# Matmul with layer norm: row tiles of A loaded as 64 KB pieces with rows 32 s + r on partition r, so that the block transposes write contiguously

## The chip, the core and the metric

The kernel runs on one core of one Trainium2 chip. The metric is the device time of one execution in microseconds (us), lower is better. The times shown are three runs of the kernel before, and one execution under the hardware profiler, from which all durations come.

## The reference

```python
m, k, n = 2048, 2048, 2048            # a, b, gamma, beta: float32
x = np.matmul(a, b)
mean = np.mean(x, axis=-1, keepdims=True)
var = np.var(x, axis=-1, keepdims=True)
normalized = (x - mean) / np.sqrt(var + eps)
return (gamma * normalized + beta).astype(np.float32)
```

Every row of the product is normalised over its 2048 columns.

## The kernel before

**Tiling.** A has 16 row tiles of 128 rows (i = 0 to 15), K has 16 tiles of 128 (kt), and the 2048 columns of the product are four blocks of 512 (q), each of them one PSUM bank. TensorE multiplies in fp16 (L132): the stationary operand is a 128x128 piece of A transposed, `at[i][:, kt, :]`, the moving one is `b16[:, kt, 512 columns]`. A tile of `at` has K on its partitions: partition p and index kt = 4c + t stand for k = 512 c + 4 p + t. B is loaded in the same order (`b_rows`, L65), so that a partition reads contiguous memory.

**The first four row tiles** (L257 to L363) are worked on while B arrives, K in two halves and the columns in two halves. Their A comes in 16 pieces of 256 KB (`load_first`, L88), is cast by VectorE (`cast_first`), turned by TensorE (`turn_first`) and copied out of PSUM by VectorE (`keep_first`). B comes in 32 pieces of 512 KB, cast half by VectorE and half by ScalarE. ScalarE puts the first half of a sum aside (`put_by`, L144), and VectorE adds the second half to it (`add_up`, L148).

**Row tiles 4 to 15** (L353 to L386) take another way for A, the one that is changed. `load_tile` (L108) loads half a row tile into a float32 buffer of [128, 8, 128] of the pool `firstp`, which has four buffers. One transfer goes to each of the four groups q of 32 partitions. In the view `a_pieces` (L66) the rows of a tile are split as 4 r + j with r on the partition; group q of 32 partitions holds columns 128 q to 128 q + 127 of each of the four stretches of 512 columns (c). Half h holds rows j = 2h and 2h + 1, all four c. ScalarE casts the half to fp16 (`cast_tile`, L116). VectorE's 32x32 block transposes (`transpose_part`, L123), four for each row tile, each with 512 elements on 128 partitions, turn it into `at[i]`: inside a group of 32 partitions a block of 32 rows by 32 columns is turned, the columns being every fourth one. Part j reads row j of every r and writes every fourth element of `at[i]`, over all 16 kt.

**Order of the work.** The order on every engine is the order of the program text (`manual_schedule`, L219): no planner changes it, and each engine works through its list in order. In the loop over row tiles (L370 to L385) VectorE does, for each tile i: the normalisation of tile i - 1 (`normalise`: `centre`, L165, reads the product in PSUM and frees the bank; `scale`, L171), then four times the statistics of a bank (`stats`, L140) followed by one transpose for tile i + 2, and up to i = 11 half of the normalisation of one of the first four tiles. PSUM has eight banks, so the banks of tile i are those of tile i - 2.

**Queues.** SP's queue carries first the pieces of A and B, then the halves of tiles 4 and 5 (L248 to L250), then gamma and beta (L251, L252), then the output (L192). The queue of GpSimd (POOL) carries the halves of tiles 6 to 15 (L253 to L255); each waits until the cast of an earlier tile has freed a buffer. In the compiled program the transfers of a queue go round over eight completion semaphores; a transfer waits for the one eight places before it to have landed.

Of the kernel before, what the change touches and what calls it, by code (L numbers as in the profile page):

```python
# [9 lines left out]
FP32 = mybir.dt.float32  # L10
# [5 lines left out]
def kernel(  # L16
# [18 lines left out]
    nc = tc.nc  # L35
    P = 128
    M, K = a.shape
    _, N = b.shape
# [10 lines left out]
    firstp = ctx.enter_context(tc.tile_pool(name="firstp", bufs=4))  # L49
# [13 lines left out]
    b16 = bpool.tile([P, n_kt, N], FP16)  # L63

    b_rows = b.rearrange("(c p t) n -> c t p n", p=P, t=4)  # L65
    a_pieces = a.rearrange("(i r j) (c q k) -> q i r (j c) k", r=32, j=4, c=4, q=4)  # L66

    bnst, x_of, mv_of, rs_of, at = {}, {}, {}, {}, {}
    a_in, b_in, t_of, tile_in, part = {}, {}, {}, {}, {}
# [36 lines left out]
        nc.vector.tensor_copy(at[g][:, ds(4 * c, 4), :], t_of[n])  # L106

    def load_tile(i, h, queue):  # L108
        f = firstp.tile([P, 8, P], FP32, tag="first", name=f"p{i}_{h}")
        for q in range(4):  # L110
            queue.dma_start(f[ds(32 * q, 32)], a_pieces[q, i][:, ds(8 * h, 8)])  # L111
        tile_in[i, h] = f

    def cast_tile(i, h):
        a16 = a16p.tile([P, 2, 4, P], FP16, tag="a16", name=f"a{i}_{h}")
        nc.scalar.copy(a16.rearrange("p j c k -> p (j c) k"), tile_in.pop((i, h)))  # L116
        tile_in[i, h] = a16

    def new_at(i):
        at[i] = atp.tile([P, n_kt, P], FP16, tag="at", name=f"at{i}")  # L120

    def transpose_part(i, j):
        nc.vector.transpose(  # L123
            at[i].rearrange("p ct (r j) -> p j ct r", j=4)[:, j],
            tile_in[i, j // 2][:, j % 2].rearrange("p c (k t) -> p c t k", t=4),
        )

    def bank(i, q):
# [90 lines left out]
    with tc.manual_schedule(engines=order):  # L219
# [28 lines left out]
        for i in (4, 5):  # L248
            for h in (0, 1):
                load_tile(i, h, nc.sync)  # L250
        nc.sync.dma_start(gamma_b, gamma.unsqueeze(0).to_broadcast([P, N]))  # L251
        nc.sync.dma_start(beta_b, beta.unsqueeze(0).to_broadcast([P, N]))  # L252
        for i in range(6, n_mt):  # L253
            for h in (0, 1):
                load_tile(i, h, nc.gpsimd)  # L255
# [13 lines left out]
        for n in range(KH):  # L269
            g, c = pieces[n]  # L270
# [83 lines left out]
        for h in (0, 1):  # L354
            cast_tile(4, h)
            transpose_part(4, 2 * h)
            transpose_part(4, 2 * h + 1)
# [7 lines left out]
        for c in range(4):  # L365
            if c % 2 == 0:
                cast_tile(5, c // 2)
            transpose_part(5, c)

        for i in range(G, n_mt):  # L370
            if i > G:
                normalise(i - 1)
            if i + 2 < n_mt:
                new_at(i + 2)
            for q in range(n_nb):
                bank(i, q)
                for t in range(n_kt):
                    mm(i, q, t)
                stats(i, q)
                if i + 2 < n_mt:  # L380
                    if q % 2 == 0:
                        cast_tile(i + 2, q // 2)
                    transpose_part(i + 2, q)
                if q == 3 and i < 3 * G:
                    normalise((i - G) // 2, (i - G) % 2)  # L385
# [32 lines left out]
```

## Time and profile before

| what | before |
|---|---|
| three runs | 252.91, 253.35, 253.96 us; median 253.35 us |
| profiled execution | 251.89 us, of which the span from the first to the last instruction is 250.1 us |
| TensorE (PE) busy | 233.6 us, 93% of the span, 1108 matmuls |
| VectorE (DVE) busy | 214.0 us, 86%, 354 instructions |
| ScalarE (ACT) busy | 58.4 us, 23% |
| GpSimd (POOL) busy | 49.2 us, 20% |
| transposes of L123 | 48, 1.28 to 1.35 us each |
| DMA | 52.6 MB, 210 GB/s over the span |

The page gives busy times of the engines, a picture of the span in 40 slices in which each digit is the busy share in tenths, and the chain of waits that ended last. The timeline of an engine has one line for an instruction or for some alike: start in us, length in us, engine, line of the code, operation, output <- inputs, shape, count, and in square brackets how long the engine had been idle and what ended that. An engine called SPq is SP's queue, and its lines are issues of transfers. Consecutive instructions of an engine overlap a little, so the distance between two starts is less than the length of one.

### The profile page before, as it was taken

The numbers are of one execution on the slowest core, as the hardware profiler recorded it, in microseconds if no ns is written. First come the engines' busy times: TensorE is split into PE (matmuls) and PEld (weight loads), VectorE is DVE, ScalarE is ACT, GpSimd is POOL, SyncE is SP. The second block draws the span as 40 slices with busy tenths as digits, with TensorE's granted clock in tenths as the row PEclk, the third lists the DMA queues.
The fourth block names the chain that finished last, engine by engine and source line by source line (L and its number), as shares of the span: only waits on it lengthen the run. The fifth ranks groups of instructions, "written<-read, shape, count | busy, mean of one in ns | idle before, by whom it ended". The sixth has DMA issues, their size and how long they took to land.

```text
span 250.1 us, 3093 instructions
## 1 busy us (share of the span) xinstructions
PE 233.6 (93%) x1108; PEld 106.4 (43%) x1108; DVE 214.0 (86%) x354; ACT 58.4 (23%) x91; POOL 49.2 (20%) x87
## 2 busy tenths in 40 slices
PE   7999999999999999999999999989979899999940
PEld 2444454444444444444444444434434344444410
DVE  1654454389999999999999999999999999999953
ACT  2225628542411321030300303011030303000010
POOL 0000000000722907051150703407042000000003
PEclk9999999999999999999999999999999999999996
DMA  6999999999999836458282852908448240404214
GB/s 196 393 390 401 402 404 408 409 368 172 226 281 235 211 95 226 145 201 221 86 235 101 241 178 109 308 33 238 154 161 259 88 168 3 168 0 168 120 48 168
DMA packets 20302, 52.62 MB, mean 210 GB/s; under 512 B 2880, under 2 KB 6976, under 8 KB 20032
## 3 DMA queue, kind: packets, MB, share of 16 engines
q1 hardware_dynamic: 16160, 41.16, 46.1%
q0 software_dynamic: 3840, 10.49, 16.7%
q10 hardware_dynamic: 288, 0.79, 0.9%
q8 instruction: 8, 0.13, 0.2%
q14 instruction: 6, 0.05, 0.1%
HBM read 35.65 MB, written 16.78 MB: 210 GB/s over the span
## 4 chain that ended last, share of the span: by engine, by line
DVE 56%; PE 28%; DMA 8%; issue 3%; ACT 2%; SPq 0%; DVEq 0%
DMA w_1_137<-in_b_dram 3%; DMA f_1_121<-in_a_dram 3%; DMA f_0_107<-in_a_dram 2%; DVE at_1489 L123 2%; DVE at_1259 L123 2%; DVE at_1719 L123 2%; DVE at_911 L123 2%; DVE at_1601 L123 2%; DVE at_1141 L123 2%; DVE at_1371 L123 2%; DVE at_1029 L123 2%; DVE at_861 L123 2%; DVE at_902 L123 2%; PE ps_0_1936 L132 1%; PE ps_3_2189 L132 1%
## 5 line engine op out<-in xcount | busy, mean ns | idle before, releaser
L111 POOL DMA_DIRECT2D p_0_221<-in_a_dram x4 | 2.5, 624 | 61.8 <-DMA p_0_209<-in_a_dram 61.8
L205 POOL TENSOR_TENSOR y_last<-y_last,gamma_b 128x512 f32<-128x512 f32 x1 | 1.3, 1266 | 54.2 <-ACT y_last L204 54.2
L132 PEld LDWEIGHTS <-at_1601 128*128 128x128 f16 x64 | 6.3, 98 | 9.1 <-issue 1.6
L132 PEld LDWEIGHTS <-at_1489 128*128 128x128 f16 x64 | 6.3, 98 | 8.7 <-issue 1.2
L132 PEld LDWEIGHTS <-at_1719 128*128 128x128 f16 x64 | 6.3, 98 | 8.7 <-issue 1.2
L132 PEld LDWEIGHTS <-at_1371 128*128 128x128 f16 x64 | 6.3, 98 | 8.0 <-issue 0.6
L132 PEld LDWEIGHTS <-at_911 128*128 128x128 f16 x64 | 6.3, 98 | 7.5
L132 PEld LDWEIGHTS <-at_1259 128*128 128x128 f16 x64 | 6.3, 98 | 7.5
L132 PEld LDWEIGHTS <-at_1935 128*128 128x128 f16 x64 | 6.3, 98 | 7.5
L132 PEld LDWEIGHTS <-at_902 128*128 128x128 f16 x64 | 6.3, 98 | 7.5
L132 PEld LDWEIGHTS <-at_1831 128*128 128x128 f16 x64 | 6.3, 98 | 7.5
L132 PEld LDWEIGHTS <-at_861 128*128 128x128 f16 x64 | 6.3, 98 | 7.5
L132 PEld LDWEIGHTS <-at_1141 128*128 128x128 f16 x64 | 6.3, 98 | 7.5
L132 PEld LDWEIGHTS <-at_1029 128*128 128x128 f16 x64 | 6.2, 98 | 7.6
L132 PEld LDWEIGHTS <-at_324 128*128 128x128 f16 x64 | 6.2, 98 | 7.5 <-issue 0.4
L132 PEld LDWEIGHTS <-at_323 128*128 128x128 f16 x64 | 6.2, 98 | 7.3
L132 PEld LDWEIGHTS <-at_322 128*128 128x128 f16 x64 | 6.2, 98 | 7.3
L227 PE MATMUL w_ps<-warm 128*128 128x512 f16 x20 | 7.4, 514 | 1.2 <-DVE warm L220 1.2
L132 PEld LDWEIGHTS <-at_321 128*128 128x128 f16 x64 | 5.9, 98 | 6.1 <-issue 0.7
L132 PE MATMUL ps_0_1832<-b_93,at_1601 128*128 128x512 f16 x16 | 3.6, 378 | 1.3 <-DVE u_0_1702 L165 1.3
L132 PE MATMUL ps_0_1720<-b_93,at_1489 128*128 128x512 f16 x16 | 3.6, 379 | 1.0 <-DVE u_0_1584 L165 1.0
L132 PE MATMUL ps_0_1936<-b_93,at_1719 128*128 128x512 f16 x16 | 3.6, 379 | 1.0 <-DVE u_0_1814 L165 1.0
(556 smaller groups left out, 613.5 us busy)
## 6 DMA issues: line engine op xcount, KB each, us to landing
gamma_b<-in_gamma_dram SPq DMA_DIRECT2D x1, 1024.0 KB, 10.5
beta_b<-in_beta_dram SPq DMA_DIRECT2D x1, 1024.0 KB, 15.6
w_0_105<-in_b_dram ACTq DMA_DIRECT2D x1, 512.0 KB, 5.1
w_0_111<-in_b_dram SPq DMA_DIRECT2D x1, 512.0 KB, 6.9
w_0_115<-in_b_dram SPq DMA_DIRECT2D x1, 512.0 KB, 7.8
w_0_119<-in_b_dram SPq DMA_DIRECT2D x1, 512.0 KB, 6.5
w_0_123<-in_b_dram SPq DMA_DIRECT2D x1, 512.0 KB, 7.5
w_0_127<-in_b_dram SPq DMA_DIRECT2D x1, 512.0 KB, 8.3
```

Source lines behind the costliest of these rows:

```text
L111: queue.dma_start(f[ds(32 * q, 32)], a_pieces[q, i][:, ds(8 * h, 8)])
L123: nc.vector.transpose(at[i].rearrange("p ct (r j) -> p j ct r", j=4)[:, j], tile_in[i, j // 2][:, j % 2].rearrange("p c (k t) -> p c t k", ...
L132: nc.tensor.matmul(x_of[i, q], at[i][:, kt, :], b16[:, kt, ds(q * NB, NB)], start=(kt == lo), stop=(kt == hi - 1),)
L205: nc.gpsimd.tensor_tensor(y, y, gamma_b[:, q3], AluOp.mult)
L227: nc.tensor.matmul(w_ps, warm[:, 0:P], warm, start=True, stop=True)
```

## The change

Rows of a tile are split as 32 s + r instead of 4 r + j, with r on the partition as before. Half h of a tile now holds stretches c = 2h and 2h + 1 of the columns, with all four s, instead of two values of j with all four c. The rows s and the stretches c don't merge into one dimension of the view, so each transfer brings one c: eight transfers of 64 KB for a half, instead of four of 128 KB; the contiguous piece in memory is 512 B in both. That makes 32 transfers instead of 16 on SP's queue and 160 instead of 80 on GpSimd's. A transpose now works on one c with all four s, reads with the same step of four elements as before, and writes runs of 32 adjacent elements; it fills four kt of `at[i]`, where a part before filled a quarter of every kt. The number of casts and transposes, their sizes and their places in the order stay.

```diff
-    a_pieces = a.rearrange("(i r j) (c q k) -> q i r (j c) k", r=32, j=4, c=4, q=4)
+    a_pieces = a.rearrange("(s r) (c q k) -> q c r s k", r=32, c=4, q=4)
...
     def load_tile(i, h, queue):
-        f = firstp.tile([P, 8, P], FP32, tag="first", name=f"p{i}_{h}")
-        for q in range(4):
-            queue.dma_start(f[ds(32 * q, 32)], a_pieces[q, i][:, ds(8 * h, 8)])
+        f = firstp.tile([P, 2, 4, P], FP32, tag="first", name=f"p{i}_{h}")
+        for c in (0, 1):
+            for q in range(4):
+                queue.dma_start(
+                    f[ds(32 * q, 32), c], a_pieces[q, 2 * h + c][:, ds(4 * i, 4)])
         tile_in[i, h] = f
 
     def cast_tile(i, h):
         a16 = a16p.tile([P, 2, 4, P], FP16, tag="a16", name=f"a{i}_{h}")
-        nc.scalar.copy(a16.rearrange("p j c k -> p (j c) k"), tile_in.pop((i, h)))
+        nc.scalar.copy(a16, tile_in.pop((i, h)))
         tile_in[i, h] = a16
...
-    def transpose_part(i, j):
+    def transpose_part(i, c):
         nc.vector.transpose(
-            at[i].rearrange("p ct (r j) -> p j ct r", j=4)[:, j],
-            tile_in[i, j // 2][:, j % 2].rearrange("p c (k t) -> p c t k", t=4),
+            at[i][:, ds(4 * c, 4), :].rearrange("p t (j r) -> p j t r", r=32),
+            tile_in[i, c // 2][:, c % 2].rearrange("p j (k t) -> p j t k", t=4),
         )
```

## The prediction

> **What bounds the kernel now.** I read first the busy rows of the page, then the timeline of TensorE (PE), then the chain of waits and the timeline of VectorE (DVE), last the queues that bring A. [...] The sum is made against the span and carried over to the median as a difference in us.
>
> ```profile
> PE   7999999999999999999999999989979899999940
> DVE  1654454389999999999999999999999999999953
> ```
>
> Both engines are full from slice 10 on (a slice is 6.25 us), so the busy rows don't say which one limits. TensorE's few 8s and the 7 after slice 10 lie between 150 and 200 us. The timeline of TensorE, one line per PSUM bank (start, length, engine, line, operation, idle time before it), shows what the dips are:
>
> ```profile
> 149.76 3.62 PE L132 MATMUL ps_3_1552<-b_93,at_1259 128*128 128x512 f16 x16
> 153.65 3.61 PE L132 MATMUL ps_0_1602<-b_93,at_1371 128*128 128x512 f16 x16 [0.27 <-DVE u_0_1472 L165]
> ...
> 164.00 3.62 PE L132 MATMUL ps_3_1664<-b_93,at_1371 128*128 128x512 f16 x16
> 168.58 3.61 PE L132 MATMUL ps_0_1720<-b_93,at_1489 128*128 128x512 f16 x16 [0.96 <-DVE u_0_1584 L165]
> ...
> 178.94 3.62 PE L132 MATMUL ps_3_1782<-b_93,at_1489 128*128 128x512 f16 x16
> 183.90 3.61 PE L132 MATMUL ps_0_1832<-b_93,at_1601 128*128 128x512 f16 x16 [1.34 <-DVE u_0_1702 L165]
> ...
> 194.25 3.62 PE L132 MATMUL ps_3_1894<-b_93,at_1601 128*128 128x512 f16 x16
> 198.83 3.40 PE L132 MATMUL ps_0_1936<-b_93,at_1719 128*128 128x512 f16 x15 [0.96 <-DVE u_0_1814 L165]
> ```
>
> Undisturbed banks start 3.453 us apart (13.81 us a row tile). The four starts shown are later than that by 0.44, 1.13, 1.51 and 1.13 us: **4.2 us in all**. Each time TensorE waits for VectorE's `centre` (L165) of the row tile two before, which frees the first of eight banks. The starts of that instruction lie at 92.37, 107.30, 122.60, 137.54, 152.84, 167.78, 183.09 and 198.03 us: 15.1 us a tile against TensorE's 13.8. So VectorE is the slower engine from about 90 to 198 us, uses up TensorE's lead of two tiles by 153 us, and from then on sets the pace. Before 153 and after 199 us TensorE runs on without a gap (3.45 us a bank up to 240.4). The whole that a faster VectorE can win is those 4.2 us.
>
> ```profile
> 158.19 0.69 DVE L140 BATCH_NORM_STATS2 bnst_1507<-ps_0_1490 128x6 f32<-128x512 f32 x1
> 158.80 1.30 DVE L123 STREAM_TRANSPOSE at_1489<-a_0_1509 128x512 f16<-128x512 f16 x1
> 159.91 0.64 DVE L140 BATCH_NORM_STATS2 bnst_1507<-ps_1_1512 128x6 f32<-128x512 f32 x1
> 160.46 1.30 DVE L123 STREAM_TRANSPOSE at_1489<-a_0_1509 128x512 f16<-128x512 f16 x1
> ```
>
> VectorE's timeline: a transpose of 512 elements takes 1.30 us. In the chain of waits four back to back take 4.68 us (1.17 each), two statistics over as many elements 1.19 us (0.595 each). A transpose costs twice an ordinary pass, about 2.2 ns an element.
>
> [...] The transposes now step 8 bytes on read and on write[...]; the trace has no transpose with one side dense. [...] in the trace the 128 KB pieces take 0.48 us of SP's queue and 0.58 us of GpSimd (POOL).
>
> **The change part by part.**
>
> *Transposes* (48 for tiles 4 to 15; 40 of them, for tiles 4 to 13, before 198 us). Output becomes dense in runs of 32 elements; input step and element count stay. The saving s per transpose is not shown. Upper bound: the pace of statistics, 1.17 - 0.595 = 0.575 us. Lower bound: 0, if the read stream alone sets the rate (a loss beyond 0.02 us I exclude, since nothing gets sparser). [...] **I take 0.13 us**[...]: VectorE arrives 40 x 0.13 = 5.2 us earlier at 198 us.
>
> *Loads of tiles 4 and 5 (SP).* 16 transfers of 128 KB become 32 of 64 KB. In the compiled program SP's transfers go round over eight completion semaphores, each waiting for the one eight places before it. Before, the two halves of tile 4 are eight transfers, and their last waits only for the last piece of B. Now the first half alone is eight, and the second half waits for the first.
>
> ```profile
> 48.84 4.16 SPq L111 DMA_DIRECT2D p_0_199<-in_a_dram  x4
> 53.96 6.82 SPq L111 DMA_DIRECT2D p_1_204<-in_a_dram  x4
> ...
> 62.04 1.05 ACT L116 CAST a_0_862<-p_0_199 128x1024 f16<-128x1024 f32 x1 [0.94 <-DMA p_0_199<-in_a_dram]
> 64.48 1.05 ACT L116 CAST a_1_866<-p_1_204 128x1024 f16<-128x1024 f32 x1 [1.39 <-DMA p_1_204<-in_a_dram]
> ...
> 66.09 2.50 DVE L123 STREAM_TRANSPOSE at_861<-a_1_866 128x512 f16<-128x512 f16 x2
> ```
>
> Let T be the landing of B's last piece, 60.5 us now; it fell behind by some 2.5 us (its last two pieces came 2.4 and 2.7 us apart, earlier ones 1.3) while pieces of A were queued, and with half of those bytes I put T at 59.2, or 60.5 at worst. The eighth piece of the first half is issued at T, lands about 3 us later (128 KB took 3.9): cast by T + 4.1 = 63.3, in time for 63.8. The second half: eight issues x 0.48 = 3.9 us, 0.4 for the start, 2.6 to land: T + 6.9 = 66.1, cast by 67.2 instead of being ready before 66.09. VectorE, in order, waits; it ends the four transposes at 67.2 + 2 x (1.17 - s) = 69.55 - 2s instead of 68.4. **Delay d = 1.15 - 2s, 0.9 us at s = 0.13; at worst (T = 60.5) 2.4 - 2s.** Behind that wait are `add_up` (L148), which frees TensorE's next bank (done at 69.1, needed at 70.33: 1.2 us of slack) and all later work of VectorE. Tile 5, gamma and beta come some 8 us later in SP's queue; gamma and beta landed at 75.4 and 81.3 and are first read at 89.4 and 90.8, tile 5 is read at 77.9: estimated T + 16 = 75 for it, gamma and beta about 81 and 87. Hidden, narrowly.
>
> *Loads of tiles 6 to 15 (POOL).* 80 issues of 0.584 us become 160. If the price stays, 9.3 us per tile beside 13.8 us; if it halves with the bytes, 4.7. Each half waits for the half before through the same kind of rotation. In the steady stage hidden: a buffer is freed at 154.1 us and its new content cast some 30 us later, and issue plus landing (4 to 6 us a piece) take 15. Contention of POOL with VectorE: none seen, passes at 154.9 (POOL busy) and 166.2 us (idle) take 0.75 and 0.75. First tiles: tile 6's second half was cast at 81.77, its transpose is at 86.4; now I put its landing at 83 to 87.
>
> *Cast on ScalarE (L116):* same 1024 elements, 1.03 us; nothing, ScalarE is 23% busy.
>
> *Sum.* VectorE gains 5.2 - 0.9 = 4.3 us by 198 us, TensorE can use 4.2. With T at its worst it is 5.2 - 2.1 = 3.1. I take 3.95 between: span 246.1, **time 253.35 - 3.95 = 249.4 us.** Full gain needs 40s > 4.2 + d, so s above 0.13; break-even s is about 0.03.
>
> **Rivals.**
> 1. *The read stream sets the transposes' rate* (s below 0.03). [...] Then only the delay at tile 4 is left; VectorE has no idle time from 57 to 198 us to absorb it, so the end moves by d = 1.15 to 2.4, say 1.65: **255.0 us**, slower. It decides when 40s is under d.
> 2. *A partial gain* (s of 0.03 to 0.10): 40s - d, about 1.3 at 0.06: **252 us**.
> 3. *Loads get late although transposes are faster*: tile 6's second half at 87 or later costs VectorE about 1.5 us more; 5.2 - 0.9 - 1.5 = 2.8: **250.5 us**. Against it: TensorE needs tile 6 only at 97.96.
> 4. *The change doesn't take effect* (transpose and loads as before): 253.35; not possible, as the patterns in the program differ.
>
> **Chances.** Forecast 0.50, rival 1 0.32, rival 2 0.10, rival 3 0.08. The measurement can tell 0.5% (1.3 us) from nothing. Faster: 0.50 + 0.08 + half of rival 2 = 0.63. Slower: three fifths of rival 1 (d over 1.3) = 0.20. Same: 0.17. Range 248.9 (full 4.2 and a little) to 255.3 (most of rival 1); within the likeliest case alone 248.9 to 250.4.
>
> **What would show it.** Mean of L123: 1.17 or less confirms the first step, 1.30 rival 1. TensorE's four waits for L165 gone, or longer. VectorE idle before the third transpose of tile 4 (66 to 68 us) for about 1 us. POOL's busy time 50 to 100 us with no wait of ScalarE's casts behind it after 95 us. The forecast is wrong if the transposes don't shorten, or if a cast of A waits for its load in the steady stage.

## The result, and the profile after

The kernel after takes 250.11 us, the median of four runs (249.99 to 250.25); the kernel before, beside it, 253.26 us (252.91 to 253.96). The ratio is 0.9872, with a 95% interval of 0.985 to 0.9894: a gain of 3.15 us, where 3.95 us were predicted. The profiled execution after took 250.16 us and has a span of 248.3 us. The profiled execution of before (251.89 us, span 250.1 us) lay 1.4 us below the median of its kernel, so the two spans differ by only 1.8 us.

The page of the kernel after, its busy times and two rows of the span in 40 slices:

```profile
PE 232.5 (94%) x1108; PEld 106.1 (43%) x1108; DVE 193.0 (78%) x354; ACT 59.0 (24%) x91; POOL 89.9 (36%) x167
...
PE   6999898999999999999999999999999999999920
...
DVE  1653455369899799998999899998999894929371
```

VectorE does the same 354 instructions in 21 us less (214.0 before), and its row has gaps where it was full. TensorE's row is full from slice 8 on; the dips between 150 and 200 us are gone. TensorE's timeline at the places shown of before, the last bank of a row tile and the first of the next (start, length, engine, line, operation), shows why:

```profile
150.94 3.62 PE L134 MATMUL ps_3_1648<-b_93,at_1355 128*128 128x512 f16 x16
154.39 3.62 PE L134 MATMUL ps_0_1698<-b_93,at_1467 128*128 128x512 f16 x16
...
164.75 3.62 PE L134 MATMUL ps_3_1760<-b_93,at_1467 128*128 128x512 f16 x16
168.21 3.62 PE L134 MATMUL ps_0_1816<-b_93,at_1585 128*128 128x512 f16 x16
...
192.38 3.62 PE L134 MATMUL ps_3_1990<-b_93,at_1697 128*128 128x512 f16 x16
195.83 3.62 PE L134 MATMUL ps_0_2032<-b_93,at_1815 128*128 128x512 f16 x16
```

Every distance is 3.45 or 3.46 us and no line has a bracket: TensorE waits for no `centre`. From the first bank of row tile 4 to the last bank of row tile 15 it needs 162.31 us (71.51 to 233.82, starts of both banks), before 166.48 us (70.33 to 236.81): **4.17 us less**. VectorE's timeline in the same stretch, statistics and transposes in turn:

```profile
151.24 0.69 DVE L125 STREAM_TRANSPOSE at_1585<-a_0_1605 128x512 f16<-128x512 f16 x1
151.85 0.66 DVE L142 BATCH_NORM_STATS2 bnst_1603<-ps_1_1608 128x6 f32<-128x512 f32 x1
152.44 0.68 DVE L125 STREAM_TRANSPOSE at_1585<-a_0_1605 128x512 f16<-128x512 f16 x1
...
154.59 0.70 DVE L142 BATCH_NORM_STATS2 bnst_1603<-ps_3_1648 128x6 f32<-128x512 f32 x1 [0.28 <-PE ps_3_1648 L134]
```

A transpose takes 0.69 us instead of 1.30, and the next instruction starts 0.61 us after it: near the pace of the statistics over as many elements (0.59 us from 151.85 to 152.44). The bracket shows who waits now: VectorE, for TensorE's bank.

The loads of row tile 4, in the timeline after: SP's issues, ScalarE's casts, VectorE's transposes.

```profile
49.74 10.55 SPq L112 DMA_DIRECT2D p_0_199<-in_a_dram  x8
60.34 3.75 SPq L112 DMA_DIRECT2D p_1_208<-in_a_dram  x8
...
62.05 1.05 ACT L118 CAST a_0_958<-p_0_199 128x1024 f16<-128x1024 f32 x1 [1.45 <-DMA p_1_208<-in_a_dram]
65.96 1.04 ACT L118 CAST a_1_962<-p_1_208 128x1024 f16<-128x1024 f32 x1 [2.86 <-DMA p_0_217<-in_a_dram]
...
65.01 1.28 DVE L125 STREAM_TRANSPOSE at_957<-a_0_958 128x512 f16<-128x512 f16 x2
67.04 1.30 DVE L125 STREAM_TRANSPOSE at_957<-a_1_962 128x512 f16<-128x512 f16 x2 [0.75 <-ACT a_1_962 L118]
```

The second half is issued only from 60.34 us on, is cast by 67.0, and VectorE waits 0.75 us for it. The last of the four transposes ends at 68.3 us all the same; before, it ended at 68.6.

So TensorE gives 4.17 us, and 3.15 arrive. The rest is at the very end. The line that ends the program has an operation named DRAIN two or three times on each engine's queue. Two rows from the view of that line, before (first fence) and after (second), show those of GpSimd's and SP's queues, three on each: shortest/median/longest in ns, then the starts of the first and the last. The longest of GpSimd's is its first; SP's first comes once the last output has landed, for which SP's queue waits 2.2 us in both.

```profile
L413 POOLq DRAIN  x3: 40/102/3592, 244.7 to 249.8; - x3
L413 SPq DRAIN  x3: 7/7/7, 249.3 to 249.6; - x3
```

```profile
L415 POOLq DRAIN  x3: 40/102/5798, 241.7 to 248.0; - x3
L415 SPq DRAIN  x3: 7/7/7, 246.3 to 247.8; - x3
```

Before, GpSimd's drain ends at 244.7 + 3.6 = 248.3 us, a microsecond ahead of SP's at 249.3: hidden. After, it ends at 241.7 + 5.8 = 247.5 us, **1.2 us behind SP's** at 246.3, and the span ends 0.8 us after the later of the two in both. 4.17 - 1.2 = 3.0 us agrees with the gain measured, 3.15 us (2.7 to 3.8 by the interval). The remaining difference of the two spans is that row tile 4 starts 1.18 us later after (71.51 against 70.33). The change doesn't make it: the same matmul of the first four row tiles, 120 before the first of row tile 4, already starts at 45.62 us against 44.43, and the first changed load is issued at 49.74 us (48.84 before). In a second profile of the kernel after (`after_again`) row tile 4 starts at 71.00 us.

### The profile page after: what moved, and what is told of

The parts are those of the page before. It is cut to its first block, busy times and chain, and to the rows that moved or that the text cites. A ratio compares the mean times of both kernels' runs of the same rounds, so it can differ in the third digit from the quotient of the medians.

```text
span 248.3 us, 3245 instructions
## 1 busy us (share of the span) xinstructions
PE 232.5 (94%) x1108; PEld 106.1 (43%) x1108; DVE 193.0 (78%) x354; ACT 59.0 (24%) x91; POOL 89.9 (36%) x167
## 4 chain that ended last, share of the span: by engine, by line
PE 77%; DMA 16%; DVE 2%; ACT 2%; issue 0%; SPq 0%
DMA w_0_169<-in_b_dram 4%; DMA w_1_153<-in_b_dram 4%; DMA w_1_137<-in_b_dram 3%; DMA f_1_121<-in_a_dram 2%; DMA f_0_107<-in_a_dram 2%; PE ps_3_2285 L134 1%; PE ps_1_2249 L134 1%; PE ps_2_2172 L134 1%; PE ps_3_2094 L134 1%; PE ps_3_1990 L134 1%; PE ps_0_1928 L134 1%; PE ps_1_1838 L134 1%; PE ps_2_1739 L134 1%; PE ps_3_1648 L134 1%; PE ps_0_1586 L134 1%; PE ps_1_1490 L134 1%
## 5 line engine op out<-in xcount | busy, mean ns | idle before, releaser
L112 POOL DMA_DIRECT2D p_0_237<-in_a_dram x8 | 4.5, 570 | 61.8 <-DMA p_1_208<-in_a_dram 61.8
L229 PE MATMUL w_ps<-warm 128*128 128x512 f16 x20 | 6.6, 465 | 1.2 <-DVE warm L222 1.2
L112 POOL DMA_DIRECT2D p_0_363<-in_a_dram x8 | 4.3, 550 | 8.0 <-ACT a_0_1605 L118 5.5
L112 POOL DMA_DIRECT2D p_0_399<-in_a_dram x8 | 4.3, 549 | 5.5 <-ACT a_0_1835 L118 5.5
L112 POOL DMA_DIRECT2D p_1_264<-in_a_dram x8 | 4.4, 549 | 4.4 <-DMA p_0_255<-in_a_dram 2.3
```

The lines of the kernel that those rows point to most:

```text
L112: queue.dma_start(f[ds(32 * q, 32), c], a_pieces[q, 2 * h + c][:, ds(4 * i, 4)])
L229: nc.tensor.matmul(w_ps, warm[:, 0:P], warm, start=True, stop=True)
```

## Experiments

Theory: dense writes alone make the transposes faster; the new loads cost nothing at row tile 4 and 1.2 us at the end, through GpSimd's drain. Rival: the loads cost through their delay at row tile 4, or nothing.

### The two halves of the change apart

`loads_only`: the new loads, with the transposes writing every fourth element.

```diff
-            at[i][:, ds(4 * c, 4), :].rearrange("p t (j r) -> p j t r", r=32),
+            at[i][:, ds(4 * c, 4), :].rearrange("p t (r j) -> p j t r", j=4),
```

> The new loads (64 KB pieces, rows 32 s + r) with the old write step of four elements in the transposes; the rows of out come out in another order inside a tile of 128, nothing else is changed. Theory (the write step alone makes the transposes slow; the doubled loads cost only the end): transposes 1.30 us, TensorE waits for L167 four or five times again, GpSimd's drain at the end about 5.8 us instead of 3.6, time 1.0 to 1.5 us above the kernel before if that drain ends last, about 254.5. As the matmuls then end late, the drain could also be hidden: it starts when GpSimd has nothing more to issue before its last two operations. Rival (the loads brought the gain): transposes well under 1.30 or time near 250.1.

`dense_old_loads`: the kernel before, with only the write side of its transposes made dense.

```diff
-            at[i].rearrange("p ct (r j) -> p j ct r", j=4)[:, j],
+            at[i].rearrange("p ct (j r) -> p j ct r", j=4)[:, j],
```

> The old loads (128 KB pieces, rows 4 r + j) with the transposes writing runs of 32 elements; the rows of out come out in another order inside a tile of 128, nothing else is changed. Theory (write step is the whole gain, and the doubled number of GpSimd's transfers costs 1.2 us at the end through its drain): transposes 0.69 us, no wait of TensorE after 60 us, drain 3.6 us and over before the last output lands, time 1.2 us below the kernel after, about 248.9. Rival (the gain of 3.15 us is all that TensorE's gaps were worth, the drain is always hidden): same time as the kernel after, 250.1.

`after_again`: the kernel after, unchanged, measured beside them.

> The kernel after, once more, to be compared on the same chip: 250.1 us, transposes 0.69 us, drain of GpSimd 5.8 us. If the start of TensorE's tile 4 (71.5 us in the kernel after, 70.3 in the kernel before) moves by about 1 us between executions of the same kernel, that difference is not the change's; if it stays at 71.5 it may be.

| kernel | median, us | ratio to before, 95% interval |
|---|---|---|
| before | 253.38 | |
| loads_only | 254.71 | 1.0062 [1.0042, 1.0082] |
| dense_old_loads | 248.44 | 0.9815 [0.9777, 0.9852] |
| after_again | 250.05 | 0.9873 [0.9843, 0.9903] |

The dense writes alone gain 4.9 us (3.7 to 5.7 by the interval; TensorE's stretch accounts for 4.2); the loads alone lose 1.3, and on top of the dense writes 1.6. (`dense_old_loads` is the fastest of these, but its rows come out in another order, so it can't stand in for the kernel after.) Where the loads lose is seen in two views of `loads_only`, TensorE's waits (instruction, what it waited for, us in total, times, longest) and the line that ends the program:

```profile
PE ps L134 <- DVE u L167: 3.5, 4, 1.3
```

```profile
L415 POOLq DRAIN  x3: 40/102/5795, 244.9 to 251.2; - x3
L415 SPq DRAIN  x3: 7/7/7, 249.5 to 250.9; - x3
```

The four waits for `centre` are back, as in before. But VectorE does the four transposes of row tile 4 in one stretch (63.97 us, 4.75 us long, no bracket), so nothing is lost to the late second half, and the first late bank starts at 153.80 us, before at 153.65. The late matmuls don't hide the drain, as the expectation allowed: it starts with GpSimd's last operation (both at 244.9 us) and ends at 250.7 us, 1.2 us after SP's. In `dense_old_loads` it is 3.59 us long again and ends at 244.7, ahead of SP's at 245.7.

### The drain at the end

`loads_on_sp`: the kernel after, with row tiles 8 to 15 loaded from SP's queue, each half behind the cast that frees a buffer; GpSimd keeps tiles 6 and 7.

```diff
-        for i in range(6, n_mt):
+        for i in (6, 7):
...
+                        if i + 4 < n_mt:
+                            load_tile(i + 4, q // 2, nc.sync)
```

> The kernel after with the loads of tiles 8 to 15 issued from SP's queue, each half right behind the cast that frees its buffer; GpSimd issues 32 transfers instead of 160. Theory (the drain grows with the number of GpSimd's transfers, 1.4 us and 28 ns for each): drain about 2.3 us, hidden behind the last output, time 248.9, 1.2 us below the kernel after. Rival (the drain does not depend on their number): drain 5.8 us, time 250.1. If SP's loads hold up its output stores, VectorE waits for buffers and the time rises above 250.1.

249.09 us, ratio 0.9835 [0.9806, 0.9863]: 0.96 us less than `after_again`, and below both kernels. The drain is hidden again, but it took 4.00 us with a fifth of the transfers, not the 2.3 us expected. So its length doesn't simply follow the count. The next four kernels vary how many transfers of 64 KB GpSimd issues, and SP's queue carries the rest (the edit against `loads_on_sp`):

```diff
-        for i in (6, 7):
+        for i in range(6, 12):
...
-                        if i + 4 < n_mt:
+                        if 12 <= i + 4 < n_mt:
```

(`gpsimd_96`; 10 for 12 in `gpsimd_64`, 13 in `gpsimd_112`; in `gpsimd_0` tiles 6 and 7 are on SP's queue too.)

> As the kernel after, but GpSimd's queue brings row tiles 6 to 11 (96 transfers of 64 KB) and SP's queue, behind the output, tiles 12 to 15. If the length of GpSimd's drain at the end follows the number of its transfers (4.00 us with 32, 5.80 with 160): 4.9 us, it ends about 0.3 to 0.5 us after SP's drain, time 249.4. If the length depends on something else (a fixed short and a fixed long value, or on how recently the last transfer was issued): 4.0 us or 5.8 us, time 249.0 or 250.1.

> As loads_on_sp, but GpSimd's queue brings row tiles 6 to 9 (64 transfers of 64 KB). The drain took 4.00 us with 32, 9.23 with 96, 5.80 with 160: between 32 and 96 a straight line gives 6.6 us, which ends about 1.5 us after SP's drain, time 250.5; if the length jumps back like between 96 and 160 it is anything from 2 to 11 us. In every case the span is to end 0.7 to 0.8 us after the later of the two drains; that is what is tested.

> As loads_on_sp, but row tiles 6 and 7 are loaded from SP's queue too, so GpSimd issues no load at all. If GpSimd's drain at the end pays only for the loads that it issued: what is left is the last tensor operation that still runs, about 1.3 us. If it has a fixed part of its own: 2 us or more. In both cases it ends before SP's drain, the span ends 0.8 us after SP's drain as in loads_on_sp, time 249.0.

> As the kernel after, but GpSimd's queue brings row tiles 6 to 12 (112 transfers of 64 KB), SP's queue tiles 13 to 15. The drain took 1.36, 4.00, 6.61 and 9.23 us with 0, 32, 64 and 96 transfers, a straight line of 0.082 us each; with 160 it took 5.80, and there GpSimd's issues show one pause of 2.50 us, ahead of the 114th. [...] with 112 there is no pause, the drain takes 1.36 + 112 x 0.082 = 10.5 us, the span ends 0.7 to 0.8 us after it, time about 255. If instead the drain pays for a share of all transfers that falls at large numbers: between 5.8 and 9.2 us, time 250 to 253.5.

All from the line that ends the program, in us; "later" is the later of the drain's end and SP's drain:

| kernel | GpSimd's transfers | drain | it ends | SP's drain | span | span - later |
|---|---|---|---|---|---|---|
| gpsimd_0 | 0 | 1.36 | 242.1 | 245.3 | 246.1 | 0.8 |
| loads_on_sp | 32 | 4.00 | 245.8 | 246.4 | 247.2 | 0.8 |
| gpsimd_64 | 64 | 6.61 | 247.7 | 245.7 | 248.5 | 0.8 |
| gpsimd_96 | 96 | 9.23 | 251.2 | 246.5 | 251.9 | 0.8 |
| gpsimd_112 | 112 | 10.53 | 253.4 | 247.4 | 254.2 | 0.8 |
| after | 160 | 5.80 | 247.5 | 246.3 | 248.3 | 0.8 |
| before | 80 of 128 KB | 3.59 | 248.3 | 249.3 | 250.1 | 0.8 |

The last column is the test: the span follows the drain wherever the drain is later, up to 6 us, and SP's where it isn't. The times follow too: one run each of `gpsimd_64` 250.28, `gpsimd_96` 253.73 and `gpsimd_112` 255.97 us, the last slower than the kernel before beside it (252.13). `gpsimd_0` took 247.84 us, before beside it 251.65; with one run each it can't be told from `loads_on_sp`.

Up to 112 transfers the length is a straight line, 1.36 us and 0.082 a transfer. None of the lengths expected for 96 came true (4.0 to 5.8); those for 64 (6.6), 0 (1.3) and 112 (10.5) did. The kernel after stands off the line. Its GpSimd timeline shows a pause at the first loads of row tile 13, which are the 113th and following:

```profile
146.93 0.55 POOL L112 DMA_DIRECT2D p_0_363<-in_a_dram  x1 [5.51 <-ACT a_0_1605 L118]
149.97 3.80 POOL L112 DMA_DIRECT2D p_0_363<-in_a_dram  x7 [2.50 <-issue]
```

2.50 us pass there in which GpSimd waits for nothing that the profile shows, ahead of the 114th transfer. Every profile with 160 transfers has this pause (2.49 or 2.50 us), those with 112 or fewer don't, and the kernels with 80 of 128 KB have one of 0.97 us ahead of the 61st. As an estimate from these figures: on the line, after's 5.80 us belongs to 54 transfers, (5.80 - 1.36) / 0.082, and if a 128 KB transfer costs the same, before's 3.59 us to 27: in both the number issued after the pause (47 and 20) and seven more. So where there is a pause, the drain's length fits the transfers behind it and not their whole number. The other 106 of after would take 8.7 us at the drain's price, and the pause is 2.50 us long. What GpSimd does in the pause and in the drain, whether bytes or transfers set the price, and what sets the place of the pause, no run here shows.

### Which side of the transpose has the price

Four kernels change the two patterns of `transpose_part` in the kernel after, with the loads as they are; x is the step in elements of 2 bytes.

```diff
-            at[i][:, ds(4 * c, 4), :].rearrange("p t (j r) -> p j t r", r=32),
-            tile_in[i, c // 2][:, c % 2].rearrange("p j (k t) -> p j t k", t=4),
+            at[i][:, ds(4 * c, 4), :].rearrange("p t m -> p (t m)").rearrange("p (b k x) -> p x b k", x=2, k=32),
+            tile_in[i, c // 2][:, c % 2].rearrange("p j m -> p (j m)").rearrange("p (x b k) -> p x b k", x=2, k=32),
```

(`write_step2`; x=8 in `write_step8`; `read_step8` has x=8 with the two patterns exchanged. `read_dense_write_step4` writes as `loads_only` does and reads `"p j (t k) -> p j t k", t=4`.)

> As the kernel after, but a transpose reads its 512 elements densely and writes them with a step of two elements (4 bytes) instead of in runs of 32; the elements of A transposed land in another order, so the product is another one. [...] 4 bytes are still at full rate: mean of the transposes 0.69 us, VectorE busy 193 us, no wait of TensorE for centre. If every step above one element costs: 1.30 us, VectorE busy 214 us, TensorE's waits for centre back, 4 us in all.

> As the kernel after, but a transpose reads its 512 elements densely and writes them with a step of four elements (8 bytes); the elements of A transposed land in another order, so the product is another one. If the write step alone sets the rate, reading at 8 bytes costing nothing in before either: mean of the transposes 1.30 us as in before. If part of before's 1.30 us was the read step: clearly below, 0.9 to 1.2 us.

> As the kernel after, but a transpose reads densely and writes with a step of eight elements (16 bytes); the elements of A transposed land in another order. [...] 16 bytes cost what 8 bytes cost: 1.30 us. If the price grows with the step [...]: above 1.8 us, VectorE busy above 238 us and the kernel some 25 us longer. If the slow case is not the write step but read and write steps together (the read is dense here): 0.69 us.

> As the kernel after, but a transpose reads with a step of eight elements (16 bytes, before it was four elements, 8 bytes) and writes densely; the elements of A transposed land in another order. If reading has no price for a step: mean of the transposes 0.69 us and the time of the kernel after, 250.1 us. [...] 1.2 to 1.3 us, VectorE busy 214 us, TensorE's waits for centre back.

Groups of instructions of `write_step8` and of `read_step8` (busy us and mean ns of one behind the bar, then idle time before them):

```profile
L125 DVE STREAM_TRANSPOSE at<-a 128x512 f16<-128x512 f16 x48 | 116.2, 2469 | 0.0
```

```profile
L125 DVE STREAM_TRANSPOSE at<-a 128x512 f16<-128x512 f16 x48 | 51.6, 1088 | 0.0
```

| kernel | read step | write step | mean, us | pace, us |
|---|---|---|---|---|
| after | 8 B | runs of 32 | 0.69 | 0.61 |
| write_step2 | dense | 4 B | 0.73 | 0.61 |
| read_dense_write_step4 | dense | 8 B | 1.30 | 1.15 |
| before | 8 B | 8 B | 1.30 | 1.15 |
| write_step8 | dense | 16 B | 2.47 | 2.28 |
| read_step8 | 16 B | dense | 1.09 | 0.98 |

The pace is the distance of starts in row tile 4's transposes: for a group of n, its length less one transpose, over n - 1; before's is the distance of the third and the fourth (66.09 and 67.24 us). Before and `read_dense_write_step4` are alike: of before's 1.30 us nothing belonged to the read step. Writing at 4 bytes costs nothing (0.61 us, as in runs of 32), and from there on the pace about doubles with the step, 1.15 and 2.28 us for 8 and 16 bytes. Reading at 8 bytes costs nothing (0.61 us) and at 16 bytes 0.37 us more. As for the times: one run each, `write_step2` (250.69 us) is like the kernel after, and `read_dense_write_step4` (254.27 us) like `loads_only`; `write_step8` (300.23) is bound by VectorE, TensorE waits 30.8 us for `centre`, and it is 50 us slower than the kernel after, where some 25 were expected. `read_step8` takes 251.94 us, before beside it 252.4. Its VectorE is busy for 209.7 us, yet no wait for `centre` is left: it loses nothing there. TensorE's last matmul ends at 239.22 us, 1.8 us later than in after (237.44), and TensorE's waits add up to 5.9 us against 4.2: 2.3 us of them are for a cast of B (L78), ahead of the transposes, for which after doesn't wait. The expectation missed: no wait came back, and a transpose took 1.09 us instead of 1.2 to 1.3.

## Why the prediction was right, and where it was off

- **The bound.** Right. TensorE's four late starts were the whole that VectorE could give: 4.2 us named, 4.17 seen.
- **Transposes, s = 0.13 us.** Mis-sized: 1.15 - 0.61 = 0.54 us, nearly the upper bound (0.575). The 0.13 us was the author's estimate between the two bounds, which nothing in the trace of before shows. The transpose's read at 8 bytes costs nothing (1.15 us of pace with the read dense and with the read at 8 bytes), and its write step has the whole price. The error hardly reached the time, since TensorE's 4.2 us was the cap: 40 s is some 22 us instead of 5.2, and VectorE spends the surplus waiting for TensorE (18.5 us in all between 71 and 240 us, none in before).
- **Delay at row tile 4.** Its times came as worked out: first half's cast at 62.05 us (T + 3 = 62.2, with T = 59.2), second half ready at 67.0 (67.2). In part two errors cancelled: B's last piece landed at 60.0 us, between the 59.2 taken and the worst case of 60.5, and the loads landed sooner than taken (2.0 us after their issue in the second half, where 2.6 was taken). The delay is 1.15 - 2s; with s measured it is nearly nil, and the last transpose ends at 68.3 us against 68.6 before.
- **Tile 5, gamma and beta.** "Hidden, narrowly" was right. Tile 5's second half landed only at 77.9 us, where 75 was estimated; its transpose starts at 79.45, without a wait; gamma and beta land at 81.6 and 86.1 (81 and 87 predicted) and are first read at 87.0 and 88.4.
- **Tile 6.** Wrong but harmless: its second half was cast from 79.79 us on, not landed at 83 to 87. Nobody waited for it, so rival 3 had no ground.
- **GpSimd's issues.** The price stays: 0.55 us for 64 KB, 0.584 for 128 KB, 89.9 us busy. "In the steady stage hidden" was right for the 160 issues themselves: no cast waits for its load after the one at 77.90 us.
- **The sum.** It failed by one term that it took as nothing: GpSimd's drain at the end, 5.80 us with 160 transfers of 64 KB and 3.59 us with 80 of 128 KB. The prediction said of GpSimd's loads only that they lie beside other work; the drain stood at the end, where nothing hid the last 1.2 us of it. 4.17 - 1.2 = 3.0 us against 3.15 measured, where the sum had 3.95. That the total came near is in part luck: the sum's own 4.3 us for VectorE, built from two wrong sizes, happened to lie at TensorE's cap, and the 0.25 us taken off for a delay that didn't come stood in for part of the missed drain.
- **Rival 1** fell: the read has no part in before's 1.30 us, which stays with the read dense. Its time of 255.0 us is what the loads cost without faster transposes, and `loads_only` took 254.71. That it fits is no support: the rival put the loss at row tile 4, where `loads_only` loses nothing, and the loss is in the drain.

## What to carry to other kernels

Read a kernel to its last line: issues that were hidden all along can come with a longer end, and it is exposed as soon as it outlasts the rest. Here GpSimd's drain of 5.80 us, after 160 transfers, ended 1.2 us behind SP's, and moving 128 of them to SP's queue gave 0.96 us. Where a strided pass costs twice an ordinary one, as here (1.15 against 0.61 us, all of it on the write side), try the dense write first, and measure the sides apart before trading one for the other. Where the resource freed is larger than the wait that it ends, size the wait, not the resource.

## What the runs showed of the hardware that was not expected

- A 32x32 block transpose of 512 fp16 elements on VectorE pays for its write step and read step differently: 8 bytes cost 1.15 against 0.61 us on the write side and nothing on the read side; 16 bytes 2.28 us on the write side, 0.98 on the read side.
- GpSimd's drain at the end grew by 0.082 us for each transfer that it had issued, up to 112 (10.53 us), though the issues of the last had ended 100 us before the drain began (142.5 and 242.9 us); with 160 it was 5.80 us, after a pause of 2.50 us in the issues.
- A transfer costs GpSimd nearly the same at half the bytes (0.55 and 0.584 us), so 160 small ones keep it busy for 89.9 us instead of 49.2.
